# One activation table loaded ahead by name, and two cache copies moved out of the attention

## The chip, the cores and the metric

The kernel runs on one core of a Trainium2 chip. The metric is the device time of one execution in microseconds (us), taken as the median of several runs; lower is better. A profile is one further execution, recorded instruction by instruction. The engines are named as the profile names them: PE (TensorE matmuls), PEld (its weight loads), DVE (VectorE), ACT (ScalarE), POOL (GpSimd), SP (SyncE, which here issues every DMA).

## The reference

One inference step of a hybrid decoder layer, for a prompt of 1024 tokens and 8 single-token samples, all in fp32 with a model width of 1024:

```
h   = rmsnorm(x) * g1
A   = swish(layernorm(causal depthwise conv31(a * sigmoid(gate))))
B   = attention, 4 heads of 64, three dilated windows joined by softmax denominators
C   = b * conv3(c * x);   D = causal pools of 2, 4, 8, 16, scaled
x   = x + [A | B | C | D] @ w_out
x   = x + (silu(h2 @ w_g) * (h2 @ w_u)) @ w_down,   h2 = rmsnorm(x) * g2
y   = rmsnorm(x) * g_final
```

For the samples the attention reads a cache of 2048 rows of K and V each. The outputs contain these caches moved on by one row, so 2047 of the 2048 rows are copied from input to output, 16 copies of 1 MB for K and 16 for V.

## The kernel before

Tokens (1024 + 8 = 1032) lie along the free axis, features on the 128 partitions. Each fp32 product is made of three fp32r matmuls of a high and a low part. The stages follow each other on PE: the input projection; the output projection, with the attention's score, transpose and value matmuls between its groups; gate and up; down, in six blocks, of which the last is `last_block`. Gate/up and the first five down blocks work on pairs of token slices with one level of Strassen's scheme. The cores of the stages are helpers, so that nearly all instructions bear the lines L369 (ACT), L376, L379, L383, L387 (DVE), L393 (POOL), L405, L411 and L419 (PE) and L428 (DMA); the tile names tell them apart.

The order on every engine is written by a list scheduler (`Sched`). Each piece of work is a generator (a stream) with a priority, which yields operations or waits for flags. The scheduler keeps a modelled clock for each engine, and one for the DMA queue, and always emits the operation that could start first, with the priority deciding among near ones. What is emitted stays in that order on its engine. A stream can wait for a modelled time, as the copies do.

The parts that the change touches:

- `copies` (L1968 on) issues the 32 copies from SP, one at a time, each 17 modelled us after the one before, from 77 on. A step that falls between 260 and 400 modelled us is put at 400.
- `sample` makes the cached attention of the 8 samples: the queries `tok` are written to DRAM (`qsd`), read back spread over the partitions (`t<-qsd`, four times), each time with three loads of cached keys (`t<-kg`), and DVE multiplies the two (`t<-t,t`, L379) and sums (`sc`, L387). These products stand in DVE's queue between those of the prompt's attention, whose mask and maximum is L1216 (the tile `M`) and sets the score banks `st` free for PE.
- `last_block` runs over four token slices x of 256, 256, 260 and 260 columns. For each slice and each of 8 row tiles m, PE makes 6 matmuls, DVE adds the bank to the residual (`g<-mm,g`, `g<-ac,g`), ACT squares it (`t<-g`) and POOL adds up the squares. Then `final(x)` calls `root`: PE sums over the partitions with a matrix of ones (`mi<-t,ones`), ACT takes a logarithm and then an exponential (first guess of 1/sqrt) and a plain scaled copy, DVE makes one Newton step of three operations (the last one writes `st`), and DVE and POOL scale the slice and SP sends it out (`out_yT`).

The activation function of each ACT instruction needs a table set in place. In the kernel before nothing is said about sets: the build puts an ACT_TABLE_LOAD ahead of an activation whose set isn't the one loaded. The root of every slice has two of them, one ahead of the logarithm and one ahead of the exponential.

Of the kernel before, what the change touches and what calls it, by code (L numbers as in the profile page):

```python
# [27 lines left out]
DBLK = [[0, 1], [2, 3], [4, 5], [6, 7], [8, 9], [10]]  # L28
# [259 lines left out]
def get(slots, **kw):  # L288
    if not slots.free:
        def cond():  # L290
            return bool(slots.free)
        cond.why = slots.tag
        while not slots.free:
            yield cond
    return slots.alloc(**kw)


def wait(cond):
    if not cond():
        yield cond  # L300
# [16 lines left out]
def emit(nc, I, O, pools):  # L317
    PLACE.clear()
    S = Sched()
# [14 lines left out]
    def has(*f):  # L334
        return lambda: all(x in flags for x in f)
# [14 lines left out]
    V, AE, GP, PE = nc.vector, nc.scalar, nc.gpsimd, nc.tensor  # L350
# [15 lines left out]
    def act(out, in_, func, **kw):  # L366
        c = (0.0525 if psum(in_) else 0.0945) + nfree(out) / 1200 + 0.093 * len(aps(kw.get("accum_out"), kw.get("bias"), kw.get("scale")))
        return Op("act", c, aps(in_, kw.get("bias"), kw.get("scale")), aps(out, kw.get("accum_out")),
                  lambda: AE.activation(out, in_, func, **kw))  # L369
# [22 lines left out]
    def ptt(out, a, b, op):  # L392
        return pool(lambda: GP.tensor_tensor(out, a, b, op), out, (a, b))  # L393
# [29 lines left out]
    def dma(out, in_, eng="sp"):  # L423
        n = 4
        for _, m in out.ap:
            n *= m
        q = {"sp": nc.sync, "act": nc.scalar, "pool": nc.gpsimd}[eng]
        return Op(eng, 0.06, (in_,), (out,), lambda: q.dma_start(out, in_), size=n, thin=nfree(out) < 512)  # L428
# [1341 lines left out]
    def calm():  # L1770

        yield from wait(lambda: S.dma < S.now + 5)
# [88 lines left out]
    def last_post(m, x, b):  # L1861
        n, q = MN[x], slice(MO[x], MO[x] + MN[x])
        yield from wait(has(("d", len(DBLK) - 2, m // 2, x // 2, m, x % 2)))
        yield tt(x2[m][:, q], b[:, 0:n], x2[m][:, q], ADD)
        MB.rel(b)
        yield from square(m, x)
# [20 lines left out]

    LW = []

    def square(m, x):  # L1890

        n, q = MN[x], slice(MO[x], MO[x] + MN[x])
        t = yield from get(TT)
        yield act(t[:, 0:n], x2[m][:, q], AF.Square)
        key = ("fin", x) + FSETS[x][m]
        if key not in ssq:
            ssq[key] = t
        else:
            yield ptt(ssq[key][:, 0:n], ssq[key][:, 0:n], t[:, 0:n], ADD)
            TT.rel(t)  # L1900
        flags.add(("f", m, x))
        if m in POOLM.get(x, ()):
            yield act(x2[m][:, q], x2[m][:, q], AF.Copy, scale=fng[:, m:m + 1])
# [64 lines left out]
    def copies():  # L1968
        t = 60.0
        for a in range(2):  # L1970
            src, dst = ((I["cache_k"], O["k_old"]), (I["cache_v"], O["v_old"]))[a]
            for n in range(8):
                L = 2047 * 256
                for o in (0, L // 2):
                    t += 17.0
                    if 260 < t < 400:
                        t = 400.0
                    yield from wait(lambda: S.clock["pe"] > t)
                    yield from calm()
                    yield dma(dst[n, o:o + L // 2].rearrange("(p e) -> p e", p=16),  # L1980
                              src[n, 256 + o:256 + o + L // 2].rearrange("(p e) -> p e", p=16))
# [14 lines left out]
    def main():  # L1996
# [20 lines left out]
        for s, cs, key in ((0, (0, 1), "out"), (1, (0, 1, 2), "out"), (0, (2,), "out2")):  # L2017
            if key == "out":
                for m in range(4 * s, 4 * s + 4):
                    t = yield from get(G, shape=[128, T])  # L2020
# [53 lines left out]
            yield from products(key, p, lambda x, j: EH[p, x][j], lambda x, j: ("e", p, x, j), gu_post(i, p), last)  # L2074
        flags.add("gu")
        MT.shut = True
        nb = len(DBLK)
        for b in range(nb - 1):
            for mp, p in [(mp, p) for mp in range(4) for p in range(2)]:
# [60 lines left out]
    S.add(3.4, "attn", attn())  # L2140
    S.add(20, "sample", sample())
    S.add(30, "copies", copies())
    S.add(100, "main", main())
    S.run()
    return S
# [95 lines left out]
```

## Time and profile before

| what | value |
|---|---|
| median of 3 runs | 1107.97 us (1106.47, 1107.97, 1112.95) |
| the profiled execution, its own time | 1112.35 us |
| its span, first to last instruction | 1110.6 us |
| mean granted TensorE clock | 0.994 of full speed |
| PE busy | 1083.6 us (98%) |
| DVE busy | 917.1 us (83%) |
| ACT busy | 512.4 us (46%) |
| POOL busy | 35.5 us (3%) |
| DMA | 205.39 MB, 185 GB/s in the mean |

The profiled execution is 4.38 us above the median and 1.75 us longer than its span. PE is busy nearly throughout, so the places where it isn't, or where its clock is lower, are few and can be named one by one; the last 11 us of the span, in which PE has nothing left to do, are the largest.

### The profile page before, as it was taken

The page shows a single profiled execution, that of the slowest core. Times are in us where ns is not written, and L with a number is a line of the kernel's source. Part 1 is how long each engine was busy: PE and PEld are TensorE (multiplying, and loading weights), DVE is VectorE, ACT ScalarE, POOL GpSimd, SP SyncE. Part 2 cuts the span into 40 slices and gives each one's busy share as a digit, 9 for nine tenths or more (in the row PEclk, how much of TensorE's full clock was granted, in tenths as well). Part 3 has the DMA queues.
Part 4 walks back from the last instruction along what each step waited for, and adds up shares of the span by engine and source line. Part 5 has one row for each costly group of instructions (what it writes and reads, how often), then busy time and mean ns, then how long its engine had stood idle before and what let it go on. Part 6 is the DMA issues. An engine that isn't in the chain of part 4 may idle for free.

```text
span 1110.6 us, 21832 instructions
## 1 busy us (share of the span) xinstructions
PE 1083.6 (98%) x8123; PEld 1050.6 (95%) x8123; DVE 917.1 (83%) x2240; ACT 512.4 (46%) x1148; POOL 35.5 (3%) x59
## 2 busy tenths in 40 slices
PE   9999999999999999999999999999999999999994
PEld 5799889998999998999999999999999999999994
DVE  5999999846855499978778887887886999999966
ACT  6553443553642255544444544543544433333346
POOL 0000000000001200000000000000000000000034
PEclk9999999999999999999999999999999999999998
DMA  8042323534467543468547646763647999693103
GB/s 300 1 164 89 117 81 126 174 121 155 153 230 245 194 162 117 154 228 276 184 150 276 210 171 230 216 203 116 210 127 265 385 363 325 236 323 126 39 12 143
DMA packets 103243, 205.39 MB, mean 185 GB/s; under 512 B 11424, under 2 KB 62928, under 8 KB 102608
## 3 DMA queue, kind: packets, MB, share of 16 engines
q1 hardware_dynamic: 103136, 203.99, 54.2%
q8 instruction: 64, 1.05, 0.4%
q14 instruction: 43, 0.35, 0.1%
HBM read 150.98 MB, written 86.87 MB: 214 GB/s over the span
## 4 chain that ended last, share of the span: by engine, by line
PE 75%; DVE 17%; DMA 3%; issue 2%; ACT 2%; POOL 0%; SPq 0%; POOLq 0%; DVEq 0%; ACTq 0%
PE mm L411 37%; PE ac L411 33%; DVE g L376 6%; DVE g L379 2%; DVE t L379 2%; DVE wo L379 2%; PE ac L405 1%; DVE ta L379 1%; DVE t L1216 1%; DVE h L379 1%; PE st L405 1%; PE st L419 1%; PE st L411 1%; ACT t L369 1%; DMA out_c_tail<-t 1%
## 5 line engine op out<-in xcount | busy, mean ns | idle before, releaser
L411 PE MATMUL mm<-h,wo 128*128 128x256 f32 (+3 forms) x2982 | 473.1, 303 | 1.9 <-DVE g L379 1.9
L411 PEld LDWEIGHTS mm<-h,wo 128*128 128x128 f32 x2982 | 428.3, 189 | 5.0 <-DVE g L379 2.1
L411 PE MATMUL ac<-h,wo 128*128 128x256 f32 (+3 forms) x1860 | 278.6, 288 | 0.1
L411 PEld LDWEIGHTS ac<-h,wo 128*128 128x128 f32 x1860 | 251.9, 189 | 0.7 <-DVE g L379 0.3
L411 PE MATMUL ac<-g,wo 128*128 128x260 f32 (+1 forms) x879 | 126.5, 282 | 1.2 <-DVE g L379 1.2
L411 PEld LDWEIGHTS ac<-g,wo 128*128 128x128 f32 x879 | 114.2, 189 | 1.4 <-DVE g L379 1.4
L379 DVE TENSOR_TENSOR g<-ac,g 128x256 f32<-128x256 f32 (+3 forms) x204 | 86.6, 427 | 29.0 <-PE ac L411 25.0
L369 ACT ACTIVATE g<-g 128x260 fp32r<-128x260 f32 (+2 forms) x201 | 74.8, 413 | 74.5 <-DVE g L379 71.9
L379 DVE TENSOR_TENSOR wo<-rw,wo 128x512 fp32r<-128x512 f32 x140 | 95.7, 689 | 15.4 <-ACT wo L369 14.7
L411 PE MATMUL mm<-g,wo 128*128 128x260 f32 (+1 forms) x735 | 107.1, 282 | 0.0
L369 ACT ACTIVATE wo<-rw 128x512 fp32r<-128x512 f32 x140 | 86.7, 624 | 31.9 <-PE mm L411 22.9
L411 PEld LDWEIGHTS mm<-g,wo 128*128 128x128 f32 x735 | 96.1, 189 | 0.0
L369 ACT ACTIVATE wo<-t 128x512 fp32r<-128x512 f32 (+1 forms) x103 | 60.8, 590 | 70.5 <-DVE t L379 52.9
L379 DVE TENSOR_TENSOR g<-g 128x260 fp32r<-128x260 f32 (+3 forms) x221 | 87.6, 422 | 4.8 <-ACT g L369 3.9
L376 DVE SCALAR_TENSOR_TENSOR g<-g,parh,g 128x384 f32<-128x384 f32 (+2 forms) x90 | 81.7, 924 | 0.5
L379 DVE TENSOR_TENSOR g<-g,g 128x256 f32<-128x256 f32 (+4 forms) x173 | 72.3, 438 | 8.7 <-ACT g L369 5.3
L379 DVE TENSOR_TENSOR g<-mm,g 128x256 f32<-128x256 f32 (+3 forms) x138 | 58.9, 429 | 20.7 <-PE mm L411 20.2
L379 DVE TENSOR_TENSOR wo<-t,wo 128x512 fp32r<-128x512 f32 (+1 forms) x103 | 65.5, 636 | 10.0 <-ACT wo L369 7.7
L369 ACT ACTIVATE t<-mm 128x256 f32<-128x256 f32 (+3 forms) x79 | 31.8, 402 | 81.2 <-PE mm L411 78.7
L369 ACT ACTIVATE t<-g 128x256 f32<-128x256 f32 (+4 forms) x90 | 39.2, 453 | 64.3 <-DVE g L379 45.2
L379 DVE TENSOR_TENSOR g<-t,g 128x260 f32<-128x260 f32 (+4 forms) x151 | 62.5, 434 | 3.7 <-ACT g L369 3.0
L369 ACT ACTIVATE g<-mm 128x260 f32<-128x260 f32 (+1 forms) x84 | 32.1, 383 | 64.8 <-PE mm L411 64.5
(167 smaller groups left out, 1230.9 us busy)
## 6 DMA issues: line engine op xcount, KB each, us to landing
hd<-g SPq DMA_DIRECT2D x74, 260.0 KB, 3.3
hd<-g SPq DMA_DIRECT2D x74, 256.0 KB, 4.4
out_k_old<-cache_k SPq DMA_DIRECT2D x16, 1023.5 KB, 6.1
out_v_old<-cache_v SPq DMA_DIRECT2D x16, 1023.5 KB, 6.7
h<-hd SPq DMA_DIRECT2D x49, 256.0 KB, 5.9
g<-w_gu SPq DMA_DIRECT2D x22, 512.0 KB, 3.6
rw<-w_gu SPq DMA_DIRECT2D x22, 512.0 KB, 4.4
h<-hd SPq DMA_DIRECT2D x40, 260.0 KB, 5.9
```

The costliest lines, as they stand in the source:

```text
L369: lambda: AE.activation(out, in_, func, **kw))
L376: return dve(lambda: V.scalar_tensor_tensor(out, a, s, b, op0, op1), out, (a, s, b), ptr=aps(s))
L379: return dve(lambda: V.tensor_tensor(out, a, b, op), out, (a, b))
L405: return Op("pe", mcost(r), (l, r), (out,), lambda: PE.matmul(out, l, r, start=start, stop=stop, skip_group_check=True))
L411: i = PE.matmul(o, l, r, start=a, stop=b, skip_group_check=True)
L419: i = PE.transpose(o, a, d)
L1216: yield dve(lambda: V.tensor_tensor_reduce(e[:, 0:w], p[:, 0:w], tab, 1.0, -3e38, ADD, MAX, m), e[:, 0:w], (p[:, 0:w], tab), extra=(m,))
```

## The change

Two edits. A new stream `table`, added when the gate/up products have been written out, waits for the first finished tile of down block 4 (the fifth, the last one ahead of `last_block`) and issues one load of the set `natural_log_exp_and_others` on ACT, with a modelled cost of 1.28 us. And the pause of the copies begins at 225 modelled us in place of 260.

```diff
     LW = []
 
+    def table():
+
+        yield from wait(has(("d", len(DBLK) - 2, 0, 0, 0, 0)))
+        yield Op("act", 1.28, (), (), lambda: AE.preload_act_table_set("natural_log_exp_and_others"))
+
     def square(m, x):
...
                     t += 17.0
-                    if 260 < t < 400:
+                    if 225 < t < 400:
                         t = 400.0
...
         MT.shut = True
+        S.add(1.5, "table", table())
         nb = len(DBLK)
```

On ACT, at the root of slice 0 (`mi` is the sum over the partitions, `g` the residual whose squares go to `t`), there stood before:

```order
L369 ACTIVATE t_426_13156<-g_88_10191 128x256
L369 ACT_TABLE_LOAD
L369 ACTIVATE t_427_13158<-mi_17_13117,eps 128x256
L369 ACT_TABLE_LOAD
L369 ACTIVATE t_427_13158<-t_427_13158 128x256
L369 ACTIVATE t_428_13159<-mi_17_13117,eps 128x256
```

and in the changed kernel at the same place:

```order
L369 ACTIVATE t_426_13157<-g_88_10191 128x256
L369 ACTIVATE t_427_13159<-mi_17_13118,eps 128x256
L369 ACTIVATE t_427_13159<-t_427_13159 128x256
L369 ACTIVATE t_428_13160<-mi_17_13118,eps 128x256
L369 ACTIVATE t_430_13175<-g_89_10196 128x256
```

Both loads are gone, and so in the other three slices: of ten loads in the program two remain, and one is new. The rest of ACT's order in `last_block` is as it was. The new load stands in down block 4, ahead of a copy of a product bank (`t<-mm`, 260 columns) and behind a split of a weight (`wo<-t`):

```order
L369 ACTIVATE wo_280_12532<-rw_67_12328 128x512
L369 ACTIVATE wo_281_12542<-t_391_12513 128x512
L1893 ACT_TABLE_LOAD
L369 ACTIVATE t_394_12577<-mm_217_12567 128x260
L369 ACTIVATE t_395_12588<-mm_218_12576 128x260
```

Nothing else moved around it. On SP, in the attention, where the sample's queries go out (`rw<-w_out` is a weight, `out_vT` an output of the prompt's values), there stood before:

```order
L428 DMA rw_17_2530<-w_out 128x1024
L428 DMA out_k_old<-cache_k 16x16376
L428 DMA qsd<-tok 8x256
L428 DMA out_vT<-t_144_2559 128x384
L428 DMA out_vT<-t_145_2592 128x256
L428 DMA t_143_2551<-qsd 128x512
L428 DMA t_146_2608<-kg 128x512
L428 DMA t_147_2632<-kg 128x512
```

and now:

```order
L428 DMA rw_17_2530<-w_out 128x1024
L428 DMA qsd<-tok 8x256
L428 DMA out_vT<-t_144_2558 128x384
L428 DMA t_143_2550<-qsd 128x512
L428 DMA t_145_2575<-kg 128x512
L428 DMA t_146_2590<-kg 128x512
L428 DMA out_vT<-t_147_2626 128x256
```

The tenth copy has gone from ahead of the queries, the eleventh, nine rows further on, has gone too; both and all that follow come two steps later behind the pause, and the last copy is at 774 modelled us in place of 740. On DVE, at the wait for the first of these keys, there stood before:

```order
L379 TENSOR_TENSOR t_144_2559<-mm_41_2511,t_27_302 128x384
L379 TENSOR_TENSOR t_146_2608<-t_146_2608,t_143_2551 128x512
L387 TENSOR_REDUCE sc<-t_146_2608 128x8
L1259 RECIPROCAL rc_0_2649<-ac_9_2442 128x3
L1216 ISA t_149_2652,M_0_2475<-st_79_2633,g_26_763 128x256
```

and now:

```order
L379 TENSOR_TENSOR t_144_2558<-mm_41_2511,t_27_302 128x384
L379 TENSOR_TENSOR t_145_2575<-t_145_2575,t_143_2550 128x512
L387 TENSOR_REDUCE sc<-t_145_2575 128x8
L379 TENSOR_TENSOR t_146_2590<-t_146_2590,t_143_2550 128x512
L387 TENSOR_REDUCE sc<-t_146_2590 128x8
L1216 ISA t_149_2645,M_0_2475<-st_78_2634,g_26_763 128x256
```

Two of the sample's products stand ahead of the prompt's maximum in place of one. From here to the end of the attention the scheduler orders PE, DVE and ACT anew (a stretch of about 140 of PE's 2141 rows); behind that, buffer numbers aside, the order is the one before but for three rows on DVE, some on ACT and SP.

## Rows read from the trace of the kernel before

**Rows 1.** Stretches: PE, PEld, DVE, ACT, POOL busy (count), PE clock, DMA share, GB/s.
```profile
250.00:275.00 25.00, 22.56 (x143) 21.74 (x142) 17.27 (x48) 10.13 (x20) 0.00 (x0) 0.93 0.43 146
700.00:800.00 100.00, 100.00 (x845) 100.00 (x845) 80.89 (x185) 46.38 (x111) 0.00 (x0) 1.00 0.60 191
1062.00:1111.00 49.00, 32.69 (x234) 30.20 (x232) 32.56 (x78) 31.32 (x62) 22.17 (x30) 0.90 0.24 87
```

**Rows 2.** PE's waits, whole span: total us, times, longest.
```profile
PE mi L405 <- POOL t L393: 3.2, 2, 1.8
PE st L411 <- DVE M L1216: 2.7, 2, 2.4
```

**Rows 3.** Stretches behind two of PE's waits, columns as in rows 1.
```profile
254.00:256.00 2.00, 2.00 (x10) 1.89 (x9) 1.93 (x8) 1.70 (x4) 0.00 (x0) 0.63 0.00 0
256.00:258.00 2.00, 2.00 (x8) 1.91 (x8) 2.00 (x4) 1.34 (x3) 0.00 (x0) 0.51 0.27 57
1080.00:1084.00 4.00, 4.00 (x21) 3.82 (x20) 3.79 (x11) 3.33 (x7) 3.64 (x5) 0.57 0.38 131
```

**Rows 4.** Timeline, attention: start, us, instruction [idle before <-releaser]; SPq is issue.
```profile
238.12 0.52 SPq L428 DMA_DIRECT2D out_k_old<-cache_k  x1
238.97 0.30 SPq L428 DMA_DIRECT2D qsd<-tok  x1
...
246.98 0.33 SPq L428 DMA_DIRECT2D t<-qsd  x1
...
251.74 0.69 DVE L379 TENSOR_TENSOR t<-t,t 128x512 f32<-128x512 f32 x1 [10.94 <-DMA t<-kg]
...
253.62 0.62 PE L411 MATMUL st<-g,g 128*128 128x384 f32 x2 [2.44 <-DVE M L1216]
```

**Rows 5.** DMA issues of small writes: count, KB each, median us to landing.
```profile
out_a_tail<-t SPq DMA_DIRECT2D x2, 19.0 KB, 5.7
...
out_c_tail<-t SPq DMA_DIRECT2D x2, 5.0 KB, 2.0
```

**Rows 6.** Groups by line, ACT: busy us, mean ns, idle before.
```profile
L369 ACT ACT_TABLE_LOAD x10 | 12.8, 1283 | 5.5 <-DMA g<-xT 5.3
```

**Rows 7.** Timeline, root of slice 0.
```profile
1073.60 1.28 ACT L369 ACT_TABLE_LOAD   x1
...
1076.68 0.42 ACT L369 ACTIVATE t<-t 128x256 f32<-128x256 f32 x1
...
1077.20 0.43 DVE L379 TENSOR_TENSOR t<-t 128x256 f32<-128x256 f32 x1 [2.06 <-ACT t L369]
...
1079.42 0.63 PE L411 MATMUL mm<-h,wo 128*128 128x260 f32 x3 [1.92 <-DVE g L379]
```

**Rows 8.** Timeline, root of slice 1, and PE's wait for POOL behind it.
```profile
1086.13 0.42 ACT L369 ACTIVATE t<-t 128x256 f32<-128x256 f32 x1
...
1086.65 0.43 DVE L379 TENSOR_TENSOR t<-t 128x256 f32<-128x256 f32 x1 [0.15 <-ACT t L369]
...
1089.95 1.14 PE L405 MATMUL mi<-t,ones 128*128 128x260 f32 x4 [1.41 <-POOL t L393]
```

**Rows 9.** Timeline, roots of slices 2 and 3.
```profile
1094.81 0.43 DVE L379 TENSOR_TENSOR t<-t 128x260 f32<-128x260 f32 x1 [1.43 <-ACT t L369]
...
1096.83 3.14 PE L405 MATMUL mi<-t,ones 128*128 128x260 f32 x10 [1.80 <-POOL t L393]
...
1097.66 0.41 DVE L379 TENSOR_TENSOR g<-ac,g 128x260 f32<-128x260 f32 x1
...
1100.39 0.48 ACT L369 ACTIVATE t<-mi,eps 128x260 f32<-128x260 f32 x1
1100.88 1.28 ACT L369 ACT_TABLE_LOAD   x1
1102.18 0.42 ACT L369 ACTIVATE t<-t 128x260 f32<-128x260 f32 x1
```

**Rows 10.** Timeline, ACT at the new load's place.
```profile
1030.50 0.39 ACT L369 ACTIVATE t<-mm 128x260 f32<-128x260 f32 x1 [2.80 <-PE mm L411]
```

## The prediction

> **What bounds the kernel now.** I first read the busy times by stretch. Outside two places PE is busy nearly all the time, as in the row of 700 to 800 us, so what it computes sets the time and the change, which leaves the matmuls alone, can only win or lose where PE idles or runs at the lower clock. The two places are 250 to 275 us, where PE idles 2.44 us and the mean clock is 0.93, and the last block from 1062 us on, where PE is busy 32.69 of 49 us [rows 1]. PE's waits name the causes: the score banks that DVE's maximum has to free, and the sum matmuls that wait for POOL's sums of squares [rows 2]. Two dips of the clock stand right behind waits: 0.63 and 0.51 in the two stretches of 2 us from 254 on, and 0.57 over 1080 to 1084 [rows 3], which is near the lower of the two levels (1.2 of 2.4 GHz). What a dip costs where PE is fully busy: (1 - 0.63) x 2 + (1 - 0.51) x 2 = 1.72 us for the first, (1 - 0.57) x 4 = 1.72 us for the second.
>
> **The copies.** The tenth copy is issued at 238.12, just ahead of the sample's queries at 238.97; the read-back of the queries can be issued only when that small write has landed, at 246.98, 8.01 us after its issue; the first product starts at 251.74, 4.76 us after the read-back's issue, DVE having idled 10.94 us [rows 4]. Behind that product in DVE's queue stands the prompt's maximum, PE runs out of score banks and idles 2.44 us [rows 4], and the dip of 1.72 us follows. Without the copy the write is a small one behind a weight of 512 KB; such small writes landed after 2.0 and 5.7 us [rows 5]. At 5.7 the read-back goes out at 244.7 and the product can start at 249.4, 2.3 us earlier than before; at 2.0 it is 6.0 us earlier. Against that, two products with their sums now stand ahead of the maximum, where it was one: 0.69 us for the further product and as much for its sum, 1.4 us in all. PE's wait becomes 2.44 - 2.3 + 1.4 = 1.5 us in the bad case and nothing in the good one. I take nothing, being nearer to the middle of the two (about 4.2 us earlier, less 1.4, more than the 2.44 needed), and with the wait the dip goes: gain 2.44 + 1.72 = 4.16 us, and 0.9 us in the bad case, where the dip comes all the same. What is late next is only PE's own work, which is the same. From here to the attention's end the order on PE, DVE and ACT is a new one; before it had one wait over 1 us in this stretch. I see no reason for a sign, so I add 0 and leave up to 4.16 us (one new wait of that kind) for the range.
>
> The copies behind the pause keep their times, one each 17 us, with two more at the end. There PE is fully busy with DMA at 0.60 [rows 1], and the weights are loaded ahead; two more copies cost nothing there as long as a weight isn't late, and were one late, PE would wait a microsecond or two.
>
> **The new load.** It stands behind a weight's split and ahead of a copy that waits for PE anyway: ACT idles 2.80 us ahead of the copy at 1030.50 [rows 10], and a load takes 1.283 us [rows 6]. It is hidden with 1.5 us to spare; without that cover it would cost its 1.28 us in one place.
>
> **The eight loads that go.** Each takes 1.28 us, and the next activation starts 1.30 us after the load's start (1100.88 to 1102.18) [rows 9]. All eight make 10.3 us of ACT, of which the path gets back less. Slice by slice, always with the ACT, DVE and PE orders of the last block, which stay:
>
> Slice 0. The exponential starts at 1076.68, DVE has then been idle for 2.06 us and PE idles 1.92 us until 1079.42, since the bank it needs is freed by an evacuation behind DVE's Newton step [rows 7]. Without the two loads, 2.6 us, the exponential is early enough, and DVE can start right behind its previous evacuation: 2.06 us. PE's wait goes, and with it probably the dip that follows.
>
> Slice 1. DVE is busy 3.79 of 4 us before this root [rows 3] and its Newton step, at 1086.65, came only 0.15 us after it had nothing left [rows 8]. So two loads give little here: 0.21 idle in that stretch, 0.15 at the step, some in between. I take 0.7, which makes 2.8 us in all. PE's next wait, 1.41 us for POOL at 1089.95 [rows 8], goes with it, since POOL waits for squares that stand behind these loads on ACT.
>
> Slice 2. DVE idles 1.43 us before its step at 1094.81 [rows 9]; with the two waits above gone its inputs are there earlier still, and of the two loads' 2.6 us I take 2.3, up to the point where the evacuations PE feeds bind. In all 5.1. The last evacuation, at 1097.66 [rows 9], stands behind this step on DVE and moves with it. PE has the room: 1.92 and 1.41 us of waits and 1.72 of the dip make 5.05.
>
> Slice 3. The last sum matmul ends at 1096.83 + 3.14 = 1099.97, the logarithm starts at 1100.39, the exponential at 1102.18 [rows 9]. Without loads the logarithm starts about 0.1 us after the sum and the exponential 0.49 us behind it, as the load does now (1100.39 to 1100.88), so at 1100.56: 1.6 us. In all 6.7.
>
> Behind it stand the Newton step, the scaling and the last output, the same as before; slices 2 and 3 now follow each other more closely at the output. I take 6.5 for such small losses. Bounds: from below what each of slice 0 and slice 3 shows on its own, 2.06 + 1.6 = 3.7; from above all eight loads, 10.3.
>
> The Trainium skill, "ScalarE: Activation LUTs", section "What ACT_TABLE_LOAD costs", gives about 2.66 us for a switch, a load of 1.283 and a drain of 1.38. The trace agrees with the load and shows no such drain, 1.30 us from the start of the load to the next activation. By the page's figure the estimate of the gain would be 6.5 x 2.66 / 1.30 = 13.3 us; the new load would still fit into its 2.80 us.
>
> **The sum.** Profiled execution 1112.35 - 6.5 - 4.16 + 0 = 1101.7. The median of the runs is 1107.97, 4.38 below the profiled one, and the runs spread by 6.5 us. The attention's wait with its dip hangs on when a small write lands and is of just that size, so I take it that the median run doesn't have it; then the median becomes 1107.97 - 6.5 = 1101.5. I forecast 1101.5.
>
> The Trainium skill, "TensorE: Matmul & The Clock Gate", Part 1, says that the clock follows how busy the array has recently been and that the count of slow matmuls varies from run to run. Here the waits of 2.44 and 1.92 us have a dip behind them and the one of 1.80 hasn't, which agrees. By that rule a dip alone, 1.72 us, may be in a run or not, on either side of the forecast.
>
> **Rivals.**
> A further gain: the median run too has the attention's wait and dip, and loses them: 1107.97 - 6.5 - 4.16 = 1097.3. For it speaks that the order is fixed and the copy always stands ahead of the queries; against it that one run is at 1106.47, below what one would then expect beside 1112.35.
> A new wait in the reordered attention: a late load of keys, now with two products ahead of the maximum, costs one wait and one dip: 1101.5 + 4.16 = 1105.7. For it speaks that DVE's queue is tight; against it, that only loads of the sample and weights are left on the queue there.
> The loads were mostly hidden: POOL's chains of adds and DVE take their place, and only slices 0 and 3 give what they show: 1107.97 - 3.7 = 1104.3. For it speaks that DVE and POOL are nearly full in 1080 to 1084 (3.79 and 3.64 of 4) [rows 3]; against it, PE's waits for POOL come from squares that ACT delivers late.
> Slower: the queries are read back four times, each with three loads of keys, and each time DVE's queue is held until the keys land. If the new order puts the products too early every time, each round costs 2.44 + 1.72 = 4.16. Two rounds eat the gain; from three on the kernel is slower, 1101.5 + 12.5 = 1114.0. Against it: in the kernel before the one long wait of the four is the one behind a copy.
> That the change doesn't do what it says, a load set again by the build, is ruled out by ACT's order, which has none behind the new one.
>
> **How the numbers follow.** What a measurement of this kernel can tell from no change is 0.5%, 5.5 us: faster means below 1102.4, slower above 1113.5. Forecast 0.60, with a range of its own from 1099 to 1104, some 0.7 of it below 1102.4; the further gain 0.13; a new wait 0.14; mostly hidden 0.08; slower 0.05. Faster 0.42 + 0.13 = 0.55 and a little of the others, 0.57; slower 0.05; within 0.5% 0.38. The range of 8 in 10 goes from 1096.5 to 1106, which takes in the forecast, the further gain, one new wait and the hidden loads, and leaves out the slower case and mixtures.
>
> **What would show it.** Right: ACT has three loads, one of them near 1024 us; in the last block PE's waits of 1.92 and 1.41 us and the dip of 1080 are gone or under 0.5 us; from the last sum matmul's end to the exponential it is about 0.6 us in place of 2.21; the first keys' product starts by 249.4 and PE's wait of 2.44 is gone, with the clock at 1.00 there. Wrong: a new wait of PE over 1.5 us between 225 and 350; or PE still waiting for POOL in the last block by as much; or a wait in down block 4 at the new load.

## The result, and the profile after

The changed kernel takes 1100.42 us (median of 5 runs, 1099.30 to 1101.13), the kernel before 1108.44 us (5 runs, 1106.47 to 1112.95). The ratio is 0.9916, with a 95% interval of 0.9894 to 0.9938: about 8 us faster. The profiled execution took 1099.81 us with a span of 1098.03, 12.54 us below the span before. That is 4.5 us more than the medians differ by, so the two profiles must not be taken for the change alone; where the 12.54 us lie is told below.

Busy time by stretch in the changed kernel (columns as in [rows 1], the last block now from 1060 on):

```profile
250.00:275.00 25.00, 24.50 (x171) 23.42 (x170) 19.09 (x49) 10.37 (x21) 0.00 (x0) 1.00 0.36 116
700.00:800.00 100.00, 100.00 (x844) 100.00 (x844) 80.54 (x183) 46.10 (x111) 0.00 (x0) 1.00 0.62 211
1060.00:1099.00 39.00, 27.57 (x203) 24.92 (x201) 28.93 (x70) 20.84 (x54) 22.16 (x30) 0.91 0.31 110
```

In the attention's stretch PE idles 0.50 us in place of 2.44 and the granted clock is 1.00, 700 to 800 us is as full as before at 211 GB/s in place of 191, and the last stretch is shorter by a fifth. ACT's loads, by groups:

```profile
L369 ACT ACT_TABLE_LOAD x2 | 2.6, 1283 | 4.6 <-DMA g<-xT 4.6
L1893 ACT ACT_TABLE_LOAD x1 | 1.3, 1283 | 0.0
```

The timeline of the changed kernel: the sample's queries and the first product, the new load, then the roots of the four slices (they answer to [rows 4], [rows 10] and [rows 7 to 9]):

```profile
236.69 0.29 SPq L428 DMA_DIRECT2D qsd<-tok  x1
...
238.55 0.36 SPq L428 DMA_DIRECT2D out_vT<-t  x1
239.01 0.38 SPq L428 DMA_DIRECT2D t<-qsd  x1
...
243.77 0.69 DVE L379 TENSOR_TENSOR t<-t,t 128x512 f32<-128x512 f32 x1 [5.25 <-DMA t<-kg]
...
1022.21 1.28 ACT L1893 ACT_TABLE_LOAD   x1
1024.95 0.39 ACT L369 ACTIVATE t<-mm 128x260 f32<-128x260 f32 x1 [1.46 <-PE mm L411]
...
1068.48 0.42 ACT L369 ACTIVATE t<-t 128x256 f32<-128x256 f32 x1
...
1069.36 0.41 DVE L379 TENSOR_TENSOR t<-t 128x256 f32<-128x256 f32 x1
...
1071.99 0.63 PE L411 MATMUL mm<-h,wo 128*128 128x260 f32 x3 [0.18 <-DVE g L379]
...
1075.01 0.70 PE L405 MATMUL mi<-t,ones 128*128 128x256 f32 x2 [0.59 <-POOL t L393]
...
1078.26 0.46 DVE L379 TENSOR_TENSOR t<-t 128x256 f32<-128x256 f32 x1
...
1084.40 0.42 DVE L379 TENSOR_TENSOR t<-t 128x260 f32<-128x260 f32 x1
...
1087.09 2.00 PE L405 MATMUL mi<-t,ones 128*128 128x260 f32 x6 [0.17 <-ACT t L369]
...
1089.12 0.48 ACT L369 ACTIVATE t<-mi,eps 128x260 f32<-128x260 f32 x1 [0.93 <-PE mi L405]
1089.63 0.42 ACT L369 ACTIVATE t<-t 128x260 f32<-128x260 f32 x1
```

The read-back of the queries goes out 2.32 us after their write (8.01 before), and PE waits 0.3 us at most from there to gate/up. Behind the new load ACT still idles 1.46 us. In the last block PE's wait at slice 0 is 0.18 us (1.92 before), the longest one left is 0.59 us for POOL at slice 1's sums, and from the end of the last sum matmul, 1087.09 + 2.00 = 1089.09, to the exponential it is 0.54 us (2.21 before).

To compare executions I cut the span into four parts, at ACT's copy of the queries (`tok`), at ACT's second table load (the start of gate/up), and at the first matmul group of the last block (1064.67 and 1058.94 us). In us, from the timelines of the executions that bear on the two edits:

| profiled execution | start to queries | to gate/up | to last block | last block |
|---|---|---|---|---|
| before | 238.68 | 178.18 | 647.8 | 45.9 |
| before, again (e3) | 239.13 | 175.60 | 647.6 | 45.9 |
| new load alone (e1) | 238.01 | 174.82 | 647.9 | 39.1 |
| earlier pause alone (e2) | 238.21 | 174.83 | 648.0 | 46.5 |
| changed | 236.39 | 174.15 | 648.4 | 39.1 |
| changed, again (e8) | 238.06 | 173.78 | 648.3 | 39.1 |
| changed, with a copy ahead of the queries (e4) | 237.76 | 177.09 | 648.8 | 39.1 |

So between the first two profiles that were compared, 6.8 us came from the last block, 4.0 from the attention, 2.3 from a start that the change doesn't touch, and 0.6 was lost in between. By the other two profiles of the old order in the attention (e3 and e1, 175.60 and 174.82), the attention gives only 0.7 to 1.5 us, and e2, which has the new order, takes as long there as e1, which has the old one. The start differs from one execution of the same kernel to the next: e8 is the changed kernel again, and takes 1.67 us more to the same point.

### The profile page after: what moved, and what is told of

Read it like the earlier page. It is cut to its first block, busy times and chain, and to the rows that moved or that the text cites. A ratio compares the mean times of both kernels' runs of the same rounds, so it can differ in the third digit from the quotient of the medians.

```text
span 1098.0 us, 21833 instructions
## 1 busy us (share of the span) xinstructions
PE 1079.6 (98%) x8123; PEld 1047.0 (95%) x8123; DVE 916.4 (83%) x2240; ACT 503.3 (46%) x1141; POOL 35.6 (3%) x59
## 4 chain that ended last, share of the span: by engine, by line
PE 76%; DVE 16%; issue 3%; DMA 2%; ACT 2%; POOL 1%; SPq 0%; POOLq 0%; DVEq 0%; ACTq 0%
PE mm L411 39%; PE ac L411 32%; DVE g L376 5%; DVE g L379 3%; DVE t L379 2%; DVE wo L379 2%; PE st L411 1%; DVE h L379 1%; PE ac L405 1%; PE st L405 1%; DVE t L1216 1%; DVE ta L379 1%; PE st L419 1%; ACT t L369 1%; DMA hd<-g 1%
## 5 line engine op out<-in xcount | busy, mean ns | idle before, releaser
L369 ACT ACTIVATE t<-g 128x256 f32<-128x256 f32 (+4 forms) x90 | 39.1, 453 | 56.7 <-DVE g L379 39.0
L411 PE MATMUL ac<-ta,wo 128*128 128x256 f32 (+1 forms) x357 | 61.9, 282 | 0.8 <-DVE g L379 0.8
```

The source lines that it names most:

```text
L411: i = PE.matmul(o, l, r, start=a, stop=b, skip_group_check=True)
```

## The experiments

**Each edit alone (e1, e2).** For e1 the pause's bound is set back, for e2 the stream isn't added. Both keep the order of every engine as it was in the kernel before (e1) or in the changed one (e2), but for the loads.

```diff
-                    if 225 < t < 400:
+                    if 260 < t < 400:
```
```diff
-        S.add(1.5, "table", table())
```

> The kernel before with the new load alone; the copies pause from 260 on as before, and every engine's order is the one before but for the loads. Theory (the eight loads stood on the path of the last block): from the last block's first matmul to the end 39.1 us in place of 45.9, median 6.5 to 6.9 us below the kernel before, about 1101.7; in the attention the wait of about 2.4 us for the score banks with its clock dip can still be there. Rival (the loads were mostly hidden and the gain came from the attention): last block shorter by at most 3.7 us, median above 1104.

> The earlier pause of the copies alone, with all ten loads; every engine's order is that of the changed kernel but for the loads. Theory: the last block takes 45.9 us as before; PE's wait of 2.4 us in the attention and its dip are gone in the profile. If the kernel before has that wait in every run, the median is about 4 us lower, 1104.3; if only in some, 1 to 2 us lower, 1106.5 to 1107.5. Rival (the new order of the attention did it, or nothing did): the same 1108.4.

Measured beside 17 runs of the kernel before, at 1110.13 us: e1 1102.63 us, ratio 0.9928 (0.9912 to 0.9944); e2 1106.97 us, ratio 0.9975 (0.9963 to 0.9986). By the medians the load alone gains 7.5 us and the pause alone 3.2 us there; by the interval of e2's ratio the pause gains 1.6 to 4.1 us. The last block of e1 is 39.1 us long as foreseen, and the rival of hidden loads falls. The gain of e2 is larger than the theory's 1 to 2 us and smaller than its 4. Its product with e1's, 0.9903, lies within the interval of the changed kernel. Read the other way, the changed kernel at 0.9916 is 1.3 us better than e1 at 0.9928, with intervals that overlap; so behind the load the pause's gain is not clear of noise.

**The kernel before, once more (e3).**

> The kernel before, unchanged, profiled once more. Theory A (the wait in the attention depends on the landing of a small write and was missing in the median run): PE's wait of 2.4 us or its dip is missing here and the time is near 1108. Theory B (the order is fixed and the copy always stands ahead of the queries): the wait of 2 to 2.5 us and the dip are there again, and what differs between runs lies elsewhere, at the start, where the first input tiles land (1.36 against 0.57 us of PE's wait in the two profiles so far).

It took 1110.0 us, beside a median of 1110.13. Its timeline at the queries:

```profile
238.57 0.52 SPq L428 DMA_DIRECT2D out_k_old<-cache_k  x1
239.42 0.30 SPq L428 DMA_DIRECT2D qsd<-tok  x1
241.28 3.84 SPq L428 DMA_DIRECT2D out_vT<-t  x2
245.23 0.38 SPq L428 DMA_DIRECT2D t<-qsd  x1
...
249.98 0.69 DVE L379 TENSOR_TENSOR t<-t,t 128x512 f32<-128x512 f32 x1 [8.72 <-DMA t<-kg]
...
251.85 0.61 PE L411 MATMUL st<-g,g 128*128 128x384 f32 x2 [0.22 <-DVE M L1216]
```

The read-back went out 5.81 us after the write in place of 8.01 [rows 4], the product started 10.85 us after the queries in place of 13.06, PE waited 0.22 us in place of 2.44, and the granted clock was 1.00 from 251 to 257 us. In e1, with the same order and copy, the read-back went out after 5.80 us and the wait was missing too. Theory A holds: the long wait is in some executions of that order and not in others, one of three profiled here.

What held the read-back in e3 was not the write, though. In SP's order the second of two outputs stands ahead of the read-back; its issue ended at 241.28 + 3.84 = 245.12, and the read-back followed 0.11 us later. In the first profile of the kernel before the same two outputs were out at 244.67, and the read-back came only 2.31 us later, at 246.98:

```profile
240.83 3.84 SPq L428 DMA_DIRECT2D out_vT<-t  x2
```

The semaphore updates in the packed traces tell the landing itself: 7.94 us after the write's issue in the first profile, 4.97 in e3 and 4.81 in e1. So in the old order a copy can hold up the read-back only when the write lands later than that output is out, 5.7 us after the write. In the new order the output stands behind the read-back.

At the start PE's wait was 0.85 us, between the two seen so far.

**The copy put back in the new order (e4).** The last copy of V is issued ahead of the queries without a modelled cost, and left out at its old place:

```diff
+        yield Op("sp", 0.06, (), (),
+                 lambda: nc.sync.dma_start(O["v_old"][7, L // 2:L].rearrange("(p e) -> p e", p=16),
+                                           I["cache_v"][7, 256 + L // 2:256 + L].rearrange("(p e) -> p e", p=16)))
         yield dma(qsd[:, :], tok)
...
+                    if a == 1 and n == 7 and o:
+                        return
```

> The changed kernel, in which the last copy of V (modelled at 774) is issued just ahead of the queries, without the scheduler knowing; the orders on all engines stay those of the changed kernel but for a swap of two rows on DVE. Theory (the copy holds up the landing of the small write and with it the keys): the read-back goes out 5 us or more later, the first keys' product starts 7 to 8 us later than in the changed kernel, PE waits 2 to 4 us for score banks and a clock dip of 1.7 us follows; median 3 to 5.5 us above the changed kernel, about 1104.5. Rival (the new order did it): no wait over 1 us, median within 0.7 us of 1100.4.

Measured 1105.28 us, ratio 0.9955 (0.9937 to 0.9972) to the kernel before in the same runs. The changed kernel at its ratio of 0.9916 would be at 1100.8 there, so the copy costs about 4.5 us in this order. Its timeline:

```profile
237.20 0.52 SPq L1283 DMA_DIRECT2D out_v_old<-cache_v  x1
238.05 0.29 SPq L428 DMA_DIRECT2D qsd<-tok  x1
...
242.88 0.32 SPq L428 DMA_DIRECT2D t<-qsd  x1
...
247.51 0.69 DVE L379 TENSOR_TENSOR t<-t,t 128x512 f32<-128x512 f32 x1 [7.62 <-DMA t<-kg]
...
248.96 0.38 ACT L369 ACTIVATE t<-mm 128x256 f32<-128x256 f32 x1 [3.08 <-DVE sc L387]
249.24 0.27 ACT L369 ACTIVATE t<-st 128x128 f32<-128x128 f32 x1
...
249.40 0.44 PE L419 MATMUL st<-prm,t 128*128 128x128 f32 x2 [2.06 <-ACT t L369]
```

and the stretch behind the wait (columns as in [rows 1]):

```profile
251.00:253.00 2.00, 2.00 (x8) 1.90 (x8) 0.97 (x4) 0.65 (x2) 0.00 (x0) 0.50 0.40 127
```

But for the copy and a swap of rows on DVE the order is that of the changed kernel, and the wait is back, 2.06 us, with the clock at 0.50 behind it. The delay and the engine differ from what was expected: the read-back went out 4.83 us after the write (landed at 4.78), the product came 2.4 us later than in the changed kernel, not 7 to 8, and PE waited not for the maximum but for ACT's copy of a score bank (`t<-st`), which stood on ACT behind a row held 3.08 us by the first product's sum on DVE. So in the new order the copy ahead of the queries makes the wait, and the order without it doesn't. The new order, with two products ahead of the maximum, is the more sensitive one in these executions: here a product 9.75 us after the queries brought the wait, in the old order one after 10.85 us (e3) didn't. So the 4.5 us are not what the copy costs in the kernel before.

**The loads put back slice by slice (e6, e9).** In `root`, the load is issued again by name ahead of the logarithm and of the exponential, for the slices named; nothing else moves.

```diff
     def root(n, out, *sets):
+        again = sets[0][0][1] == 0
...
+        def ln():
+            if again:
+                AE.preload_act_table_set("natural_log_exp_and_others")
+            return AE.activation(r_, p_, AF.Ln, scale=1.0 / D, bias=eps)
```

(and the same for the exponential; 0 is 1, 2, 3 in the others, and `in (0, 1)` in e9).

> The changed kernel with two loads put back at the root of slice 0 alone, ahead of the logarithm and of the exponential; all other orders as in the changed kernel. The prediction's step: DVE's Newton step comes 2.06 us later and PE waits about 1.9 us for the evacuation behind it; later waits of PE (0.59 and 0.43 us in the changed kernel) take some of it up, so from the last block's first matmul to the end 40.1 to 41.1 us against 39.1 (up to 42.8 with a clock dip). Rival (the loads simply add up on one chain, 2.6 us a slice): 41.7.

> As the one with slice 0, with the two loads at the root of slice 1 alone. The prediction's step: DVE is busy with evacuations and scalings there, 0.7 us, so 39.8 us against 39.1. Rival (adds up): 41.7. Rival (hidden): 39.1.

> As the one with slice 0, with the two loads at the root of slice 2 alone. The prediction's step: 2.3 us, so 41.4 us against 39.1. Rival (adds up): 41.7. Rival (hidden): 39.1.

> As the one with slice 0, with the two loads at the root of slice 3 alone. The prediction's step: the second load is exposed whole and 0.3 us of the first, 1.6 us, so 40.7 us against 39.1. Rival (adds up): 41.7. Rival (hidden): 39.1.

> The changed kernel with the loads put back at the roots of slices 0 and 1. Alone they cost 1.73 and 3.27 us (a clock dip among the latter), and all four slices together, in the kernel before, 6.81, less than the 8.73 of the four alone. Theory (the overlap lies between slices 0 and 1, whose waits of PE for POOL are the same wait): 6.81 - 2.06 - 1.67 = 3.1 us, so 42.2 us from the last block's first matmul to the end. Rival (they add up, and the overlap lies between slices 1 and 2): 5.0 us, so 44.1.

These are single executions, and the figures are lengths of the last block in their profiles.

| loads at the root of | last block, us | more than 39.09 | expected |
|---|---|---|---|
| slice 0 | 40.82 | 1.73 | 1.0 to 2.0 |
| slice 1 | 42.36 | 3.27 | 0.7 |
| slice 2 | 41.15 | 2.06 | 2.3 |
| slice 3 | 40.76 | 1.67 | 1.6 |
| slices 0 and 1 | 42.5 | 3.4 | 3.1 |
| all (before) | 45.90 | 6.81 | 6.5 to 6.7 |

Slices 0, 2 and 3 are as the steps had them, slice 1 isn't. PE's waits over 0.3 us in the last block with the loads at slice 1 alone:

```profile
1074.64 0.70 PE L405 MATMUL mi<-t,ones 128*128 128x256 f32 x2 [0.59 <-POOL t L393]
1082.14 1.94 PE L405 MATMUL mi<-t,ones 128*128 128x260 f32 x4 [2.17 <-POOL t L393]
```

and the stretch behind the second one (columns as in [rows 1]):

```profile
1082.00:1086.00 4.00, 3.86 (x15) 3.48 (x16) 2.50 (x7) 2.85 (x8) 2.31 (x5) 0.57 0.43 143
```

The loads hold up the squares on ACT, these POOL's sums, and these PE, 2.17 us, and a slow clock follows. It isn't DVE, on which the step rested, that ends this wait. Of the 3.27 us the dip accounts for about (1 - 0.57) x 4 = 1.7, an estimate; without it slice 1 would still cost about twice the 0.7 of the step. With slice 0's loads in place as well (e9) the wait for POOL is 1.64 us and has no dip behind it (granted clock 1.00 from 1086 to 1090 us); the dip stands behind slice 0's wait there (0.57 from 1076 to 1080). Both together cost 3.4 us, against 1.73 + 3.27 = 5.0 apart, so the overlap of 1.9 us between the four alone (8.73) and all together (6.81) lies mostly between these two. How much of it hangs on where the dips fell, single executions can't tell.

**Eight loads in down block 4 (e5).**

```diff
-        yield from wait(has(("d", len(DBLK) - 2, 0, 0, 0, 0)))
-        yield Op("act", 1.28, (), (), lambda: AE.preload_act_table_set("natural_log_exp_and_others"))
+        for mp in range(4):
+            for p in range(2):
+                yield from wait(has(("d", len(DBLK) - 2, mp, p, 2 * mp, 0)))
+                yield Op("act", 1.28, (), (), lambda: AE.preload_act_table_set("natural_log_exp_and_others"))
```

> The changed kernel with eight loads in down block 4 in place of one, one behind each group of products; all other orders are the same. Theory (a load there is hidden in ACT's idle time of 2 to 3 us ahead of the next bank copy): the same time within 0.5 us. Rival (a load costs its 1.28 us there too): 9 us more, 1109; by the estimate from the Trainium skill's page ScalarE: Activation LUTs, What ACT_TABLE_LOAD costs (2.66 us a switch), a load still fits, but 7 more of them would leave gaps of the copies at the slices of 256 columns too short and some PE waits would be seen.

Measured 1100.16 us against 1100.44 for the changed kernel in the same session (e8): no cost, with eight loads of 1283 ns in the trace and no wait of PE in down block 4. The cover is shown, for one load and for eight.

**The first load by name too (e7), and the changed kernel again (e8).**

```diff
+        yield Op("act", 0.01, (), (), lambda: AE.preload_act_table_set("exp_and_others"))
         yield fill(ones, 1.0)
```

> The changed kernel, in which the program's first load is also issued by name, as ACT's first instruction, ahead of the wait for the first input tile. In the changed kernel ACT waits 4.56 us for that tile, then loads for 1.28 us, and PE waits 0.57 us for the first scaled tile behind its 5 us of warming matmuls. Theory (that load stands on the path): ACT's first activation starts 1.28 us earlier, PE's wait of 0.57 to 1.4 us goes, and the median is 0.5 to 1.3 us below the changed kernel. Rival (PE waits for the following input tiles anyway): the same within 0.3 us, with the wait found again behind the first tiles.

> The changed kernel, unchanged, on the chip of the run with the first table, to compare the two there and to see how much its profile differs from one execution to the next. Ratio to the kernel before 0.989 to 0.994; PE's wait at the start between 0.5 and 1.4 us; no wait of PE over 1.5 us in the attention.

Start of the timeline of e8, the changed kernel:

```profile
4.55 1.28 ACT L369 ACT_TABLE_LOAD   x1 [4.55 <-DMA g<-xT]
5.84 1.12 ACT L369 ACTIVATE h<-g,prm 128x384 f32<-128x384 f32 x2
...
6.51 2.93 PE L405 MATMUL ac<-h,g 128*128 128x384 f32 x4 [0.56 <-ACT h L369]
```

and of e7:

```profile
0.73 1.28 ACT L2104 ACT_TABLE_LOAD   x1 [0.73 <-PEq L2224]
4.94 1.12 ACT L369 ACTIVATE h<-g,prm 128x384 f32<-128x384 f32 x2 [2.92 <-DMA g<-xT]
...
6.05 4.18 PE L405 MATMUL ac<-h,g 128*128 128x384 f32 x6
```

The load runs while the input is under way, and PE's first product starts 0.46 us earlier. e7 took 1099.18 us (ratio 0.9912, 0.9895 to 0.9930), e8 1100.44 us (0.9920, 0.9903 to 0.9936). The shift at the start is shown; that e7's median, the lowest of all versions run, is 1.26 us below e8's by this load is not, as the intervals overlap.

## Why the prediction was right, point by point

**The sum.** Forecast 1101.5, measured 1100.42, within the forecast's own range of 1099 to 1104. The two ways to it, from the profile with the wait and from a median without it, were put as equal; e3 and e1 show the second to be right for two of three profiled executions. That the figure came so near is in part luck. The gain was forecast at 6.5 us and measured at 8.0, and at 8.9 with e8 (1109.36 and 1100.44). Of what is missing 0.3 us lies in the last block; the rest is likely the attention's, which was put at nothing, but no run shows where it lies in the median. The base of 1107.97, a median of 3 runs, was lower than the medians of 5, 9 and 17 runs that followed (1108.44, 1109.36 and 1110.13), and that made up for part of it.

**The last block.** Forecast 6.5 (steps 6.7), measured 6.81, and the same to within 0.04 us in four executions without loads in the last block (changed, e1, e5, e8). The mechanism is the one described: DVE's step at slice 0 right behind its evacuation, PE's waits of 1.92, 1.41 and 1.80 us gone or under 0.5, and 0.54 us from the sum to the exponential where 0.6 was foreseen. A wait of 0.59 us for POOL at slice 1's sums is new beside the first profile, where the dip stood. The other price in the prediction, 13.3 us, is twice what was measured.

**The step that failed: slice 1.** "DVE is busy 3.79 of 4 us before this root ... So two loads give little here", 0.7 us. Alone they cost 3.27 us, by way of POOL and of the dip behind its wait. The prediction knew that POOL waits for squares behind these loads on ACT, but it took PE's wait for POOL as room only, and priced the step by DVE, the engine that follows the root. The sum came out since slice 0's wait and this one overlap, so that the share given to slice 0 held most of it: the order of the shares was wrong, their total right.

**The clock dip in the last block.** The prediction counted its 1.72 us [rows 3] among the room that PE has. In e3 the dip is missing, and the last block takes 45.88 us against 45.90: PE then waits for POOL 0.59 and 2.18 us where it waited 1.41 before. So this dip cost nothing, as PE waited for another engine at the next step. A dip elsewhere does cost: in e2 one fell on the last sum matmuls, which stand on the path to the end, and ten of them took 4.11 us in place of 3.14 [rows 9]; the last block took 46.5 us. The row from e2's timeline, and the stretch (columns as in [rows 1]):

```profile
1093.19 4.11 PE L405 MATMUL mi<-t,ones 128*128 128x260 f32 x10 [1.82 <-POOL t L393]
1093.00:1097.00 4.00, 3.81 (x10) 2.37 (x10) 4.00 (x11) 3.22 (x6) 1.57 (x3) 0.64 0.23 83
```

**The attention.** The write landed after 2.11 us and was read back after 2.32, near the good end of the bounds (2.0 and 5.7), the first product started at 243.77, and the wait and the dip were gone. What the prediction didn't see is that in the old order the second output holds the read-back until 5.8 us after the write, however early the write lands (e1, e3); the earlier read-back is owed to the new order too. What was mis-sized is what this is worth in the median: the forecast put it at nothing, e2 measured 3.2 us. The 4.5 of e4 hold for the new order and don't size it. The parts of the profiles give 0.7 to 4.0 us there. How often the kernel before has the long wait in an unprofiled run, and so why e2 gains more than its own profile shows against e3 (0.8 us), stays open.

**The new load.** As forecast, hidden with 1.46 us to spare (1.5 foreseen).

**The rivals.** A new wait in the reordered attention wasn't there: PE's longest wait between the queries and gate/up is 0.3 us in the changed kernel. The hidden loads fall by e1, the slower case with late keys by e8 and the other executions (the first product starts 7.35 to 7.56 us after the queries in all ten with no copy ahead of them). The further gain of 4.16 us is there in part, between the 1.3 us beside e1 and the 3.2 of e2.

## What to carry to other kernels

A table load costs its 1.3 us only where the engines that follow wait for that activation, or for what is queued behind it; look at every consumer of that engine's queue, not just the next one on the path, and put the load into a stretch where the engine idles. When several waits are removed at once, their shares can overlap: measure the total, and each alone before trusting the parts. A big transfer issued just ahead of a small write that something reads back is paid in the landing of the small one, unless the read-back is held up for as long by what stands ahead of it in its own queue; and one profile of a kernel whose runs spread by several us may hold a wait that the median run doesn't have.

## What the runs showed of the hardware

A write of 8 KB landed, by the semaphore updates in the traces, 1.98 to 2.17 us after its issue in the ten profiles without a copy of 1 MB just ahead, and after 4.78 (e4), 4.81 (e1), 4.97 (e3) and 7.94 us (before) with one. The granted clock was 0.57 over the 4 us behind a wait of 1.92 us in one execution of the kernel before, and 1.00 behind one of 1.88 us in another with the same order (e3). An ACT_TABLE_LOAD takes 1283 ns in all of them, also where the set it names is the one already loaded (e5), and the next activation can start 1.30 us after the load's start [rows 9].
